# Two block products of the next gate and up pair, issued before the last plain group of what precedes them

## The chip, the cores and the metric

The kernel runs on one core of a Trainium2 chip. The metric is device time in microseconds for one execution of the whole layer. Beside it stands one execution recorded by the hardware profiler. Five engines appear: TensorE (PE in the rows, and PEld for its weight loads), VectorE (DVE), ScalarE (ACT), GpSimd (POOL) and SyncE (SP). SP issues the loads from memory, POOL issues a second kind of DMA that adds one buffer to another.

## The reference

One decoder layer in float32 for 256 tokens of width 2048. It is a half step of SwiGLU, then a mixer of dilated attention and gated linear attention, then cross-attention, then a second half step of SwiGLU. The change touches the two half steps alone:

```python
def swiglu(h, w_gate, w_up, w_down):
    return (jax.nn.silu(h @ w_gate) * (h @ w_up)) @ w_down

x = x + 0.5 * swiglu(rms_norm(x, ffn1_norm[l]), ffn1_w_gate[l], ffn1_w_up[l], ffn1_w_down[l])
```

The gate and up weights are 2048 x 5632 and the down weights 5632 x 2048. The norm's gain is folded into the activations, and its per-token factor r is applied to the finished products, inside the silu and in the multiplication by the up half.

## The kernel before

**Tiles.** The 5632 hidden columns are taken in 11 blocks f of 512, and the 2048 rows in 4 groups of 512. A weight group (tile `raw`, 128 x 4 x 512, 1 MB) is loaded by SP (L132) and split into two parts: ScalarE rounds it to fp32r (`wh`, L136) and VectorE subtracts to get the remainder (`wl`, L137). TensorE then forms three products per weight, wh by the high half of the activations (L163), wl by the high half (L164), wh by the low half (L165). A plain group is 24 matmuls, for two halves of 128 tokens (`mm3`).

**Block products.** For f = 0 of a half step, gate and up are two plain projections (`proj`). For f = 1 to 10, gate and up of one block are a pair (`strassen`) that saves one of eight products on the first two weight groups of both: the left and right weight groups 0 (`ral`, `rar`) and 1 (`rbl`, `rbr`) are combined, and seven block products of 12 matmuls each (`product`, L194) stand for them. Their order is x from ral; y from ral+rar; x from the sum with rbr as well; c0l from rbl; x from rar+rbr; c0r from rbr; and, between two plain groups, x from ral+rar+rbr+rbl. Here they are called x, y, s1, c0l, s2, c0r and xb1. The sums of weights are made in place, by VectorE (`add`, L212) and by DMAs from POOL's queue (`accumulate`, L216). Between products, results in PSUM are copied or subtracted: ScalarE copies x to c0l after the first product (L228) and y to `ys` after the second (L234), VectorE subtracts for c0r after s1 (L238) and for c1r after s2 (L243). After the seven products come the plain groups 2 and 3 of gate (left) and up (right): g2l, xb1, g2r, g3l, g3r.

**Order of the work.** The program is written in this order, and a scheduler places each engine's instructions. Splits, loads and small vector operations stand under a priority (`WPRI` = 200) that lets them be placed earlier than their place in the text. Each engine runs its own list in order and waits on semaphores. What limits how far ahead a split can run are the buffers: three slots each for `wh` and `wl` (so the split of a group waits for the end of the group three before it), six for `raw` in a half step, four PSUM accumulators and four further PSUM tiles for x, y and the transposes.

**After a pair.** The silu of gate (`sg`, L377), the product with up (`h`, L387) and the eight transposes (L355, `turn`, put off by two ticks of `later`) prepare the down product. The blocks are taken in parts of 4, 4 and 3; after each part follow the down products of that part, four chunks of 512 columns with one plain group for each block, and their sums are added to the residual (L394).

Of the kernel before, what the change touches and what calls it, by code (L numbers as in the profile page):

```python
# [8 lines left out]
F32 = mybir.dt.float32  # L9
# [7 lines left out]
P = 128  # L17
# [3 lines left out]
NC = D // 512  # L21
# [6 lines left out]
WPRI = 200  # L28
# [20 lines left out]
def layer_kernel(ctx: ExitStack, tc: tile.TileContext, A: dict, out: bass.AP):  # L49
    nc = tc.nc  # L50
    V, SC, G, PE, SY = nc.vector, nc.scalar, nc.gpsimd, nc.tensor, nc.sync
# [6 lines left out]
    pa = ctx.enter_context(tc.tile_pool(name="pa", bufs=4, space=PSUM))  # L58
# [83 lines left out]
    def wgroup(W, c, g, fine=None):  # L142

        raw = load(W, c, g)
        n = W.shape[-1]
        kn = W.shape[-2]
        with tc.high_priority(WPRI):
            wh, wl = split_tiles(kn, n)
            for i in range(kn if fine else 1):
                d = slice(i, i + 1) if fine else slice(0, kn)  # L150
                if fine:
                    fine(i)
                split(wh[:, d], wl[:, d], raw[:, d])
        ks = [(kn * g + kk, wh[:, kk], wl[:, kk]) for kk in range(kn)]
        yield ks[:kn // 2]
        yield ks[kn // 2:]

    def mm3(acc, lhs, half, first, last, ts=range(TT), seeded=False):

        for t in ts:  # L160
            for i, (k, wh, wl) in enumerate(half):
                lh, ll = lhs(k, t)
                PE.matmul(acc[t], lh, wh, start=first and i == 0, stop=False, skip_group_check=seeded)  # L163
                PE.matmul(acc[t], lh, wl, start=False, stop=False, skip_group_check=seeded)  # L164
                PE.matmul(acc[t], ll, wh, start=False, stop=last and i == len(half) - 1, skip_group_check=seeded)  # L165
# [22 lines left out]
    def product(acc, lhs, w, start):  # L188

        wh, wl = w  # L190
        first = start
        for i, j, w in ((0, 0, wh), (1, 0, wh), (0, 1, wl)):
            for k in range(4):
                PE.matmul(acc, lhs(k)[i], w[:, k], start=first, stop=j == 1 and k == 3, skip_group_check=not start)  # L194
                first = False
        tick()

    def strassen(Wl, cl, Wr, cr, lhs, ab, sums, groups):

        a, b = ab  # L200
        ral, rar = load(Wl, cl, a), load(Wr, cr, a)
        rbr, rbl = load(Wr, cr, b), load(Wl, cl, b)

        def parts(src):
            with tc.high_priority(WPRI):
                wh, wl = split_tiles(4, 512)
                split(wh, wl, src)
            return wh, wl

        def add(dst, x, y):  # L210
            with tc.high_priority(WPRI):
                V.tensor_add(dst, x, y)  # L212

        def accumulate(dst, x):
            with tc.high_priority(WPRI):
                G.dma_start(dst, x, accum_op=ALU.add)  # L216

        def of(g, t):
            return lambda k: lhs(4 * g + k, t)

        def s_(i):
            return lambda k: tuple(x[:, i, k] for x in sums)

        x, y = PM([P, 512], "x"), PM([P, 512], "y")
        c0l, c0r, c1r = (pa.tile([P, 512], F32, tag="acc", name="acc") for _ in range(3))
        product(x, of(a, 0), parts(ral), True)
        with tc.high_priority(WPRI):
            SC.copy(c0l, x)  # L228
        add(ral, ral, rar)
        accumulate(rar, rbr)  # L230
        product(y, s_(0), parts(ral), True)
        with tc.high_priority(WPRI):
            ys = W2([P, 512], "ys")
            SC.copy(ys, y)  # L234
        add(ral, ral, rbr)
        product(x, s_(1), parts(ral), False)
        with tc.high_priority(WPRI):
            V.tensor_sub(c0r, ys, x)  # L238
        product(c0l, of(b, 0), parts(rbl), False)
        accumulate(ral, rbl)  # L240
        product(x, s_(2), parts(rar), False)
        with tc.high_priority(WPRI):
            V.tensor_sub(c1r, ys, x)  # L243
        product(c0r, s_(3), parts(rbr), False)
        accs = ((c0l, x), (c0r, c1r))
        for i, g in enumerate(groups):
            for acc, W, c in zip(accs, (Wl, Wr), (cl, cr)):
                for h, half in enumerate(wgroup(W, c, g)):
                    mm3(acc, lhs, half, False, i == len(groups) - 1 and h == 1, seeded=True)
                    tick()  # L250
                if i == 0 and W is Wl and c == cl:
                    product(x, of(b, 1), parts(ral), False)
        return accs

    def proj(W, c, lhs, groups, fine=None, last=False):

        n = W.shape[-1]
        acc = [pa.tile([P, n], F32, tag="acc", name="acc") for _ in range(TT)]
        groups = list(groups)
        for i, g in enumerate(groups):  # L260
            if fine and i:
                fine(4 * i)
            if last and i == len(groups) - 1:
                both = [w for half in wgroup(W, c, g) for w in half]
                for t in range(TT):
# [80 lines left out]
    def ffn(pre, r, after, fine=None, last=False):  # L346
        wg, wu, wd = (A[f"{pre}_w_{n}"] for n in ("gate", "up", "down"))
        hT = {}

        def turn(f, hs):  # L350
            hi, lo = (FT("h", 8, [P, 4, S], F32R, n) for n in ("hTh", "hTl"))
            for t in range(TT):
                tp = PM([P, 4, P], "tp")
                for j in range(4):
                    PE.transpose(tp[:, j], hs[t][:, j * P:(j + 1) * P], ident)  # L355
                sl = slice(t * P, (t + 1) * P)
                split_from_psum(hi[:, :, sl], lo[:, :, sl], tp)
# [6 lines left out]
        sums = None  # L364
        for part in PARTS:
            for f in part:
                if sums is None:
                    gate = proj(wg, f, lhs_x, range(4), fine)
                    if callable(r):
                        r = r()  # L370
                else:
                    gate, upv = strassen(wg, f, wu, f, lhs_x, (0, 1), sums, (2, 3))
                sg = []
                with tc.high_priority(WPRI):
                    for t in range(TT):
                        s = W2([P, 512], "sg")
                        SC.activation(s, gate[t], AF.Silu, scale=r[:, t:t + 1])  # L377
                        sg.append(s)
                if sums is None:
                    sums = tuple(FT(n, 1, [P, 4, 4, P], F32R, n) for n in ("sh", "sl"))  # L380
                    sums_of(xT[0], xT[1], lambda i: tuple(p[:, 2 * i:2 * i + 2] for p in sums))
                    upv = proj(wu, f, lhs_x, range(4))
                hs = []
                with tc.high_priority(WPRI):
                    for t in range(TT):
                        h = W2([P, 512], "h")
                        V.scalar_tensor_tensor(h, upv[t], r[:, t:t + 1], sg[t], op0=ALU.mult, op1=ALU.mult)  # L387
                        hs.append(h)
                later(2, lambda f=f, hs=hs: turn(f, hs))
# [256 lines left out]
    for p2 in range(2):  # L646
        acc = proj(win, 8 + p2, lhs_x, range(4))
# [18 lines left out]
    for p2 in range(2):  # L666
        acc = proj(win, 10 + p2, lhs_x, range(4))
# [183 lines left out]
    acc = proj(A["xattn_w_k"], 0, lhs_mem, range(4))  # L851
# [181 lines left out]
```

## Time and profile before

| what | us |
|---|---|
| median of 3 runs | 1958.72 (1958.36 to 1960.10) |
| profiled execution | 1957.67 |
| its span, first to last instruction | 1955.9 |
| PE busy | 1925.7 (98%) |
| DVE busy | 1261.5 (64%) |
| ACT busy | 976.7 (50%) |
| PE waiting for ScalarE's `wh`, 8 times | 15.5 |
| PE waiting for VectorE's `wl`, 17 times | 7.0 |

The first rows are one number seen in three ways: runs without the profiler, the profiled execution, and the stretch of it that the trace covers; 1.8 us of the profiled execution lie outside the span. Busy shares are averages over the whole layer. What an engine waited for is listed by the instruction that waited, the instruction that released it, the sum, the count and the longest. In a timeline a row gives the start, the length, the engine, the source line, the operation with its output and inputs, the number of instructions taken together, and in brackets the idle time ahead of it with what ended it.

### The profile page before, as it was taken

What the parts mean: (1) busy time and instruction counts of PE and PEld (TensorE: products, weight loads), DVE (VectorE), ACT (ScalarE), POOL (GpSimd) and SP (SyncE); (2) the same over time, 40 slices, a digit from 0 to 9 for tenths busy, and PEclk for the clock granted to TensorE, in tenths of its full rate; (3) what the DMA queues carried; (4) which work ended last, traced back from release to release, by engine and by line L of the source; (5) the groups of instructions that cost most, each with busy time, mean ns of one, the idle gap of its engine ahead of it and who ended that gap; (6) DMA issues with size and microseconds to landing.
All of it is one profiled execution on the core that took longest, in us unless ns stands there. A gap on an engine that the chain in (4) does not pass through costs nothing.

```text
span 1955.9 us, 21245 instructions
## 1 busy us (share of the span) xinstructions
PE 1925.7 (98%) x8760; PEld 1586.1 (81%) x8760; DVE 1261.5 (64%) x947; ACT 976.7 (50%) x876; POOL 98.1 (5%) x101
## 2 busy tenths in 40 slices
PE   8999999999999999999999999899999999999999
PEld 6888878888878888778888889788888788887887
DVE  7776467775578655446775555677746777457863
ACT  6555345553356446444566445545534555335642
POOL 2000000000000000012221000000000000000000
PEclk9999999999999999999999999899999999999999
DMA  9677557775567734445456553567755777556771
GB/s 368 234 236 258 191 146 265 273 267 192 173 222 236 281 127 161 153 169 189 172 215 215 185 182 144 204 228 248 253 193 150 258 271 267 211 177 215 237 284 60
DMA packets 63292, 416.13 MB, mean 213 GB/s; under 512 B 7099, under 2 KB 8251, under 8 KB 14428
## 3 DMA queue, kind: packets, MB, share of 16 engines
q1 hardware_dynamic: 56284, 370.74, 49.6%
q0 software_dynamic: 5760, 41.95, 10.4%
q10 hardware_dynamic: 1152, 2.10, 0.3%
q8 instruction: 68, 1.11, 0.2%
q14 instruction: 28, 0.23, 0.0%
HBM read 370.72 MB, written 2.10 MB: 191 GB/s over the span
## 4 chain that ended last, share of the span: by engine, by line
PE 74%; DVE 16%; ACT 6%; issue 4%; DMA 1%; POOL 0%; SPq 0%; ACTq 0%; DVEq 0%
PE acc L164 20%; PE acc L165 20%; PE acc L163 20%; DVE wl L137 10%; ACT wh L136 5%; PE x L194 5%; DVE raw L212 4%; PE acc L194 1%; PE x L165 1%; PE x L164 1%; PE x L163 1%; DVE h L387 1%; PE y L194 1%; DVE acc L238 1%; PE tp L315 0%
## 5 line engine op out<-in xcount | busy, mean ns | idle before, releaser
L137 DVE TENSOR_TENSOR wl<-raw,wh 128x2048 fp32r<-128x2048 f32 (+1 forms) x407 | 919.2, 2278 | 591.8 <-ACT wh L136 589.9
L136 ACT CAST wh<-raw 128x2048 fp32r<-128x2048 f32 (+1 forms) x407 | 762.4, 1898 | 656.2 <-PE acc L165 477.7
L163 PE MATMUL acc<-wh,xTh 128*128 128x512 f32 x1024 | 403.3, 395 | 15.5 <-ACT wh L136 15.5
L164 PE MATMUL acc<-wl,xTh 128*128 128x512 f32 x1024 | 402.9, 393 | 7.1 <-DVE wl L137 7.0
L165 PE MATMUL acc<-wh,xTl 128*128 128x512 f32 x1024 | 400.7, 391 | 0.0
L163 PE MATMUL acc<-wh,hTh 128*128 128x512 f32 x704 | 274.7, 390 | 0.0
L165 PE MATMUL acc<-wh,hTl 128*128 128x512 f32 x704 | 274.0, 389 | 0.0
L164 PE MATMUL acc<-wl,hTh 128*128 128x512 f32 x704 | 273.9, 389 | 0.0
L163 PEld LDWEIGHTS acc<-wh,xTh 128*128 128x128 f32 x1024 | 193.0, 189 | 59.0 <-ACT wh L136 18.6
L164 PEld LDWEIGHTS acc<-wl,xTh 128*128 128x128 f32 x1024 | 193.5, 189 | 55.4 <-DVE wl L137 16.1
L165 PEld LDWEIGHTS acc<-wh,xTl 128*128 128x128 f32 x1024 | 193.4, 189 | 39.8
L165 PEld LDWEIGHTS acc<-wh,hTl 128*128 128x128 f32 x704 | 132.1, 188 | 27.4
L164 PEld LDWEIGHTS acc<-wl,hTh 128*128 128x128 f32 x704 | 132.2, 188 | 27.3
L163 PEld LDWEIGHTS acc<-wh,hTh 128*128 128x128 f32 x704 | 132.2, 188 | 27.1
L216 POOL DMA_DIRECT2D raw<-raw x40 | 34.6, 865 | 1179.2 <-DVE raw L212 966.2
L212 DVE TENSOR_TENSOR raw<-raw 128x2048 f32<-128x2048 f32 x40 | 91.5, 2287 | 0.7
L165 PE MATMUL x<-wh,xTl 128*128 128x512 f32 x160 | 62.3, 389 | 0.0
L164 PE MATMUL x<-wl,xTh 128*128 128x512 f32 x160 | 62.3, 389 | 0.0
L163 PE MATMUL x<-wh,xTh 128*128 128x512 f32 x160 | 62.2, 389 | 0.0
L228 ACT COPY acc<-x 128x512 f32<-128x512 f32 x20 | 11.4, 571 | 95.6 <-PE x L194 95.6
L163 PE MATMUL acc<-wh,mTh 128*128 128x512 f32 x128 | 50.1, 392 | 0.0
L165 PE MATMUL acc<-wh,mTl 128*128 128x512 f32 x128 | 49.8, 389 | 0.0
(302 smaller groups left out, 1945.0 us busy)
## 6 DMA issues: line engine op xcount, KB each, us to landing
raw<-in_ffn_w_up_dram SPq DMA_DIRECT2D x88, 1024.0 KB, 7.0
raw<-in_ffn_w_down_dram SPq DMA_DIRECT2D x88, 1024.0 KB, 5.0
raw<-in_ffn_w_gate_dram SPq DMA_DIRECT2D x85, 1024.0 KB, 7.1
raw<-in_w_in_dram SPq DMA_DIRECT2D x48, 1024.0 KB, 4.8
raw<-raw POOLq DMA_DIRECT2D x40, 1024.0 KB, 6.9
raw<-in_w_out_dram SPq DMA_DIRECT2D x16, 1024.0 KB, 4.8
raw<-in_xattn_w_k_dram SPq DMA_DIRECT2D x4, 1024.0 KB, 5.6
raw<-in_xattn_w_q_dram SPq DMA_DIRECT2D x4, 1024.0 KB, 4.7
```

Of the source, the lines that this page charges most:

```text
L136: SC.copy(wh, src)
L137: V.tensor_sub(wl, src, wh.bitcast(F32))
L163: PE.matmul(acc[t], lh, wh, start=first and i == 0, stop=False, skip_group_check=seeded)
L164: PE.matmul(acc[t], lh, wl, start=False, stop=False, skip_group_check=seeded)
L165: PE.matmul(acc[t], ll, wh, start=False, stop=last and i == len(half) - 1, skip_group_check=seeded)
L194: PE.matmul(acc, lhs(k)[i], w[:, k], start=first, stop=j == 1 and k == 3, skip_group_check=not start)
L212: V.tensor_add(dst, x, y)
L216: G.dma_start(dst, x, accum_op=ALU.add)
L228: SC.copy(c0l, x)
L238: V.tensor_sub(c0r, ys, x)
L387: V.scalar_tensor_tensor(h, upv[t], r[:, t:t + 1], sg[t], op0=ALU.mult, op1=ALU.mult)
```

## The change

`strassen` is cut in two. A new function `head` issues the four loads of the pair, the products x and y, the copies that follow each of them, the first sum by VectorE and the first sum by DMA. It returns a function `rest` that issues everything else. A caller may now issue the head of the next pair early, through an argument `ahead`, just before the last plain group of what is running:

- within a part, the head of pair f+1 is issued before g3r, the last plain group of pair f;
- for f = 0, the head of pair 1 is issued before the last group of the up projection;
- at a down part that is not the last, the head of the next part's first pair is issued before the last group of the fourth chunk.

So each of the 20 heads of the layer is issued one plain group earlier. The accumulators for c0r and c1r are taken in `rest`. No product, load, sum or copy is added or removed.

```diff
     def strassen(Wl, cl, Wr, cr, lhs, ab, sums, groups):
 
+        state = head(Wl, cl, Wr, cr, lhs, ab, sums)
+        return state(groups)
+
+    def head(Wl, cl, Wr, cr, lhs, ab, sums):
+
         a, b = ab
         ral, rar = load(Wl, cl, a), load(Wr, cr, a)
         rbr, rbl = load(Wr, cr, b), load(Wl, cl, b)
...
         x, y = PM([P, 512], "x"), PM([P, 512], "y")
-        c0l, c0r, c1r = (pa.tile([P, 512], F32, tag="acc", name="acc") for _ in range(3))
+        c0l = pa.tile([P, 512], F32, tag="acc", name="acc")
         product(x, of(a, 0), parts(ral), True)
...
             SC.copy(ys, y)
-        add(ral, ral, rbr)
...
+        def rest(groups, ahead=None):
+            c0r, c1r = (pa.tile([P, 512], F32, tag="acc", name="acc") for _ in range(2))
+            add(ral, ral, rbr)
+            product(x, s_(1), parts(ral), False)
...
+            for i, g in enumerate(groups):
+                for acc, W, c in zip(accs, (Wl, Wr), (cl, cr)):
+                    if ahead and acc is accs[1] and i == len(groups) - 1:
+                        ahead()
+                    for h, half in enumerate(wgroup(W, c, g)):
...
-    def proj(W, c, lhs, groups, fine=None, last=False):
+    def proj(W, c, lhs, groups, fine=None, last=False, ahead=None):
...
         for i, g in enumerate(groups):
+            if ahead and i == len(groups) - 1:
+                ahead()
...
+        def begin(f):
+            heads[f] = head(wg, f, wu, f, lhs_x, (0, 1), sums)
+
         for part in PARTS:
             for f in part:
+                ahead = (lambda f=f: begin(f + 1)) if f + 1 in part else None
...
-                    gate, upv = strassen(wg, f, wu, f, lhs_x, (0, 1), sums, (2, 3))
+                    gate, upv = heads.pop(f)((2, 3), ahead)
...
-                    upv = proj(wu, f, lhs_x, range(4))
+                    upv = proj(wu, f, lhs_x, range(4), ahead=ahead)
...
-                acc = proj(wd, c, lhs_h, part, last=last and end and c == NC - 1)
+                ahead = (lambda: begin(part[-1] + 1)) if c == NC - 1 and not end else None
+                acc = proj(wd, c, lhs_h, part, last=last and end and c == NC - 1, ahead=ahead)
```

In the changed kernel the line numbers above 197 shift: the add is L217, the accumulating DMA L221, the copies L233 and L239, the subtractions L246 and L251, the silu L397, h L407, the transposes L369. Splits, matmuls of groups and matmuls of products keep L136, L137, L163 to L165 and L194.

Three places of the engines' lists, first before and then with the change. The first is VectorE in pair f = 6 of the first half step, from the subtraction for c0r onwards. `raw_2483` is the weight group of g2l, `raw_2353` that of the product c0r, `raw_2349` that of xb1. Before:

```order
L238 TENSOR_TENSOR acc_2360<-ys_2413,x_2357 128x512
L137 TENSOR_TENSOR wl_2451<-raw_2351,wh_2450 128x2048
L137 TENSOR_TENSOR wl_2468<-raw_2353,wh_2467 128x2048
L243 TENSOR_TENSOR acc_2361<-ys_2413,x_2357 128x512
L137 TENSOR_TENSOR wl_2486<-raw_2483,wh_2485 128x2048
L137 TENSOR_TENSOR wl_2514<-raw_2349,wh_2513 128x2048
```

With the change (`raw_2315` is here the group of the product c0r, `raw_2311` that of xb1):

```order
L137 TENSOR_TENSOR wl_2451<-raw_2313,wh_2450 128x2048
L246 TENSOR_TENSOR acc_2397<-ys_2357,x_2319 128x512
L137 TENSOR_TENSOR wl_2468<-raw_2315,wh_2467 128x2048
L137 TENSOR_TENSOR wl_2486<-raw_2483,wh_2485 128x2048
L251 TENSOR_TENSOR acc_2398<-ys_2357,x_2319 128x512
L289 TENSOR_TENSOR hTl_2434<-tp_2435,hTh_2433 128x4x128
L137 TENSOR_TENSOR wl_2514<-raw_2311,wh_2513 128x2048
```

The subtraction for c1r has moved behind the split of g2l; the same holds in all 20 pairs.

The second is TensorE in pair f = 4 of the first half step, the first pair after a down part: the end of the product c0r and the start of g2l. `wh_1929` and `wl_1930` belong to g2l, `wh_1975` to g2r. Before:

```order
L194 MATMUL acc_1820<-wl_1912,sh_321 128x512 x4
L163 MATMUL acc_1819<-wh_1929,xTh2_214 128x512
L163 MATMUL x_1817<-wh_1929,xTh2_214 128x512
L163 MATMUL acc_1820<-wh_1975,xTh2_214 128x512
L163 MATMUL acc_1821<-wh_1975,xTh2_214 128x512
L164 MATMUL acc_1819<-wl_1930,xTh2_214 128x512
```

With the change:

```order
L194 MATMUL acc_1857<-wl_1912,sh_321 128x512 x4
L163 MATMUL acc_1787<-wh_1929,xTh2_214 128x512
L164 MATMUL acc_1787<-wl_1930,xTh2_214 128x512
L165 MATMUL acc_1787<-wh_1929,xTl2_215 128x512
L163 MATMUL acc_1787<-wh_1929,xTh2_214 128x512
L164 MATMUL acc_1787<-wl_1930,xTh2_214 128x512
```

Before, two matmuls of g2r stood between the first two and the rest of g2l; now g2l, xb1 and g2r stand one after the other, whole. The same holds in the four pairs that follow a down part.

The third is ScalarE at the first pair (f = 1) of the first half step. `sg` are the silus of block 0, the copy is c0l from x. Before (`raw_463` is the sum for s1, `raw_469` the group of c0l):

```order
L136 CAST wh_530<-raw_463 128x2048
L377 ACTIVATE sg_317<-acc_128,r1_315 128x512
L377 ACTIVATE sg_319<-acc_129,r1_315 128x512
L228 COPY acc_473<-x_471 128x512
L136 CAST wh_547<-raw_469 128x2048
```

With the change (`raw_429` is the sum for s1, `raw_435` the group of c0l, `raw_431` the sum for s2, `raw_477` the last group of up):

```order
L136 CAST wh_479<-raw_477 128x2048
L136 CAST wh_514<-raw_429 128x2048
L136 CAST wh_531<-raw_435 128x2048
L318 ACTIVATE junk_307,ss1_290<-x3_106 128x512
L318 ACTIVATE junk_309,ss1_290<-x3_106 128x512
L136 CAST wh_564<-raw_431 128x2048
L397 ACTIVATE sg_317<-acc_128,r1_315 128x512
L397 ACTIVATE sg_319<-acc_129,r1_315 128x512
L233 COPY acc_439<-x_437 128x512
```

The casts for s1, c0l and s2 now all stand ahead of the two silus and the copy; before it was the cast for s1 alone.

More of the change, by code (lines that the diff above doesn't have):

```diff
@@ L234, in strassen @@
             SC.copy(ys, y)
-        add(ral, ral, rbr)
[L236 to L253, printed above, removed]
-    def proj(W, c, lhs, groups, fine=None, last=False):
+        def rest(groups, ahead=None):
+            c0r, c1r = (pa.tile([P, 512], F32, tag="acc", name="acc") for _ in range(2))
+            add(ral, ral, rbr)
+            product(x, s_(1), parts(ral), False)
+            with tc.high_priority(WPRI):
+                V.tensor_sub(c0r, ys, x)
+            product(c0l, of(b, 0), parts(rbl), False)
+            accumulate(ral, rbl)
+            product(x, s_(2), parts(rar), False)
+            with tc.high_priority(WPRI):
+                V.tensor_sub(c1r, ys, x)
+            product(c0r, s_(3), parts(rbr), False)
+            accs = ((c0l, x), (c0r, c1r))
+            for i, g in enumerate(groups):
[3 more added lines that the diff above has]
+                    for h, half in enumerate(wgroup(W, c, g)):
+                        mm3(acc, lhs, half, False, i == len(groups) - 1 and h == 1, seeded=True)
+                        tick()
+                    if i == 0 and W is Wl and c == cl:
+                        product(x, of(b, 1), parts(ral), False)
+            return accs
+        return rest
+    def proj(W, c, lhs, groups, fine=None, last=False, ahead=None):
         n = W.shape[-1]
@@ L364, in ffn @@
         sums = None
+        heads = {}
+        def begin(f):
+            heads[f] = head(wg, f, wu, f, lhs_x, (0, 1), sums)
         for part in PARTS:
             for f in part:
+                ahead = (lambda f=f: begin(f + 1)) if f + 1 in part else None
                 if sums is None:
```

## The prediction

> **What bounds the kernel now.** I read the page's busy times first, then the list of what TensorE waited for, then the timelines at those places.
>
> ```profile
> span 1955.9 us, 21245 instructions
> PE 1925.7 (98%) x8760; PEld 1586.1 (81%) x8760; DVE 1261.5 (64%) x947; ACT 976.7 (50%) x876; POOL 98.1 (5%) x101
> ...
> L137 DVE TENSOR_TENSOR wl<-raw,wh 128x2048 fp32r<-128x2048 f32 (+1 forms) x407 | 919.2, 2278 | 591.8 <-ACT wh L136 589.9
> L136 ACT CAST wh<-raw 128x2048 fp32r<-128x2048 f32 (+1 forms) x407 | 762.4, 1898 | 656.2 <-PE acc L165 477.7
> ...
> L212 DVE TENSOR_TENSOR raw<-raw 128x2048 f32<-128x2048 f32 x40 | 91.5, 2287 | 0.7
> ...
> raw<-in_ffn_w_up_dram SPq DMA_DIRECT2D x88, 1024.0 KB, 7.0
> ...
> raw<-raw POOLq DMA_DIRECT2D x40, 1024.0 KB, 6.9
> ```
>
> TensorE is busy for all but 30.2 us of the span (1955.9 - 1925.7), and the change takes no matmul away. All it can win is a part of those 30 us, and it can lose anything. A split costs 1.90 us on ScalarE and 2.28 on VectorE, an add 2.29, and the DMAs about 7 us to land.
>
> ```profile
> PE acc L163 <- ACT wh L136: 15.5, 8, 4.6
> PE acc L164 <- DVE wl L137: 7.0, 17, 2.1
> PE wps L428 <- DVE mhalf L422: 1.1, 1, 1.1
> PE tp L662 <- DVE o L677: 1.0, 1, 1.0
> PE x L194 <- ACT acc L228: 0.7, 1, 0.7
> ```
>
> Columns: total, times, longest. Three kinds of wait stand where the change moves something. The commonest is at the start of g2l, here in pair f = 6 of the first half step:
>
> ```profile
> 377.70 0.39 PE L163 MATMUL acc<-wh,xTh 128*128 128x512 f32 x1
> 377.93 0.39 PE L163 MATMUL x<-wh,xTh 128*128 128x512 f32 x1
> 378.51 0.50 PE L164 MATMUL acc<-wl,xTh 128*128 128x512 f32 x1 [0.19 <-DVE wl L137]
> 378.85 0.40 PE L165 MATMUL acc<-wh,xTl 128*128 128x512 f32 x1
> ```
> ```profile
> 371.17 4.49 DVE L137 TENSOR_TENSOR wl<-raw,wh 128x2048 fp32r<-128x2048 f32 x2
> 375.57 0.69 DVE L243 TENSOR_TENSOR acc<-ys,x 128x512 f32<-128x512 f32 x1
> 376.17 6.69 DVE L137 TENSOR_TENSOR wl<-raw,wh 128x2048 fp32r<-128x2048 f32 x3
> ```
>
> The subtraction for c1r (L243) waits for the end of product s2, and the split of g2l stands behind it in VectorE's list. The two need 0.69 + 2.28 us less a little overlap; product c0r covers 2.7. TensorE starts 0.58 us after the matmul before instead of 0.23, and the next start is 0.34 late instead of 0.23: 0.35 + 0.11 = 0.46 us lost. It recurs in 15 of the 20 pairs, nearly all of the 17 waits for `wl` above.
>
> **The change, part by part.** First, g2l. The new list has the split of g2l ahead of the c1r subtraction. Its slot in the ring is that of the product s1, three groups before, so it can be done when s1 has ended and two splits have been taken, about 2 us before TensorE needs it. Behind it the subtraction is done about 1 us later than s2 ends; who waits for it is g2r, which now starts 2.72 + 5.44 + 2.72 = 10.9 us after s2 ends. (A product is 12 matmuls, a plain group 24, at 0.227.) The stall goes whole: 15 x 0.46 = 6.9 us.
>
> Second, the pairs after a down part:
>
> ```profile
> 291.12 0.39 PE L163 MATMUL x<-wh,xTh 128*128 128x512 f32 x1
> 293.95 0.73 PE L163 MATMUL acc<-wh,xTh 128*128 128x512 f32 x2 [2.44 <-ACT wh L136]
> ...
> 551.52 0.73 PE L163 MATMUL acc<-wh,xTh 128*128 128x512 f32 x2 [1.55 <-ACT wh L136]
> ...
> 1518.90 0.72 PE L163 MATMUL acc<-wh,xTh 128*128 128x512 f32 x2 [1.52 <-ACT wh L136]
> ...
> 1776.48 0.73 PE L163 MATMUL acc<-wh,xTh 128*128 128x512 f32 x2 [1.54 <-ACT wh L136]
> ```
> ```profile
> 282.32 0.85 POOL L216 DMA_DIRECT2D raw<-raw  x1 [10.67 <-DVE wl L137]
> ```
> ```profile
> 290.19 3.71 ACT L136 CAST wh<-raw 128x2048 fp32r<-128x2048 f32 x2 [2.77 <-PE acc L194]
> ```
>
> TensorE's list has two matmuls of g2r after the first two of g2l. The cast of g2r is the second of the two in the ScalarE row, behind that of xb1. The cast of xb1 needs the sum that the DMA of 282.32 adds, which lands some 7 us later; so g2r's cast ends at 293.9. The place waits 293.95 - 291.12 - 0.23 = 2.60 us, and 0.16 over the bracketed idle at the other three: 1.71, 1.68, 1.70. With 0.11 for each restart this is 7.7 + 0.4 = 8.1 us. The new list has g2l whole, then xb1, then g2r. Even with the cast at the same moment, xb1 would have both its parts by about 294.3 and is wanted only at 290.9 + 5.4 = 296.3; g2r later still. I count all 8.1 as gained.
>
> Third, the head in its new place. Let T = 0 be the start of g3l; x' then runs from 5.44, y' from 8.16, g3r from 10.88. The slot of g3r in the ring of three is that of g3l, so its cast cannot start before 5.44; it ends at 7.4, the `wl` at 9.7, and TensorE wants it at 10.88 + 0.23 = 11.1. That is **1.3 us of cover, the smallest in the steady pair**, and it stands if VectorE is free at 7.4. Ahead of it stand the split of x', an add, the split of y' and an add, 4 x 2.29 = 9.2 us with one cast between. The slot of x' comes free at -5.4 (end of xb1), so these can be done at about 7.3. Nothing else is lost if this holds; where it doesn't, TensorE waits at every boundary. I take nothing, between 0 and the 1.1 us a head that rival (d) works out. The loads: four of the next pair now pass g3r's on SP's queue, and SP waits in order for free buffers. Walking the new lists with these durations, I get a shortest lead of about 10 us from issue to cast, against 7.0 to land, and for a POOL addition at least 4 us beyond its 6.9. I count both at nothing; without that cover the price would be the shortfall, some us each.
>
> Fourth, the first pair of the first half step, where I see a loss:
>
> ```profile
> 61.84 1.07 PE L194 MATMUL y<-wh,sh 128*128 128x512 f32 x4
> ...
> 63.65 1.07 PE L194 MATMUL y<-wl,sh 128*128 128x512 f32 x4
> 65.39 1.20 PE L194 MATMUL x<-wh,sh 128*128 128x512 f32 x4 [0.67 <-ACT acc L228]
> ```
> ```profile
> 61.79 1.91 ACT L136 CAST wh<-raw 128x2048 fp32r<-128x2048 f32 x1 [3.52 <-DVE r1t L335]
> 63.60 1.26 ACT L377 ACTIVATE sg<-acc,r 128x512 f32<-128x512 f32 x2
> 64.75 0.59 ACT L228 COPY acc<-x 128x512 f32<-128x512 f32 x1
> ```
> ```profile
> 62.05 0.71 POOL L331 TENSOR_TENSOR r<-r1m,mhalf 128x2 f32<-128x2 f32 x1 [5.45 <-DVE r1m L337]
> ```
>
> s1 overwrites x and so waits for the copy to c0l; the copy's PSUM buffer is one of gate's, so it waits for the silus, and these for r, ready at 62.76. Before, y ends at 63.65 + 0.91 = 64.56 and s1 starts at 65.39: 0.83 lost, 0.94 with the restart. Now x', y' and g3u (the last up group) end together at the same 64.56, but in the other order. ScalarE's list has the cast for s2 ahead of the silus, and the slot of that cast is g3u's: it can start only at 64.6. The silus then follow at 66.5 (a cast's step is 63.60 - 61.79 = 1.81), the copy at 67.65 (step 64.75 - 63.60), and it ends at 68.25. So s1 starts at 68.3, after **3.74 us of idleness**, 3.85 with the restart: 2.9 us worse than before. Queued behind the copy are only works for later products. The other half step has its r early, and I find no such wait there.
>
> Is the clock lost as well? The windows (PE busy, PEld, DVE, ACT, POOL, then the granted clock, DMA share, GB/s):
>
> ```profile
> 16.00:18.00 2.00, 1.22 (x2) 0.50 (x2) 1.63 (x2) 1.45 (x3) 1.04 (x1) 0.62 1.05 440
> 18.00:22.00 4.00, 2.30 (x5) 1.82 (x6) 4.00 (x5) 3.77 (x3) 0.52 (x1) 0.50 1.02 426
> 22.00:24.00 2.00, 2.00 (x8) 1.59 (x7) 2.00 (x1) 0.70 (x2) 2.00 (x2) 0.67 1.01 398
> ...
> 294.00:298.00 4.00, 4.00 (x18) 3.29 (x19) 2.63 (x2) 0.00 (x0) 0.00 (x0) 1.00 0.95 358
> ...
> 1232.00:1236.00 4.00, 0.00 (x0) 0.00 (x0) 4.00 (x9) 3.31 (x4) 0.70 (x1) 0.88 0.00 0
> 1236.00:1240.00 4.00, 1.56 (x3) 0.84 (x4) 4.00 (x4) 4.00 (x4) 0.00 (x0) 0.50 0.01 2
> ```
> ```profile
> 16.52 1.22 PE L163 MATMUL acc<-wh,xTh 128*128 128x512 f32 x2 [2.76 <-ACT wh L136]
> ```
>
> After the idle 2.44 us that end at 293.95 the clock is 1.00. After the 2.76 that end at 16.52 it falls to 0.62 and then 0.50, and after the longest wait of all, 4.6 us (1232 to 1236 is empty), it is 0.50 too. Idleness of 3.74 lies between the latter two, so I expect the fall. Its price: 4 us at 0.50 and 2 at 0.67 lose 2.0 + 0.7 = 2.7 of full-speed time by the first of them; bounds 0 and 4 (if 8 us ran at half). I take 2.5.
>
> [...]
>
> The sum against the profiled execution of 1957.67 (span 1955.9 and 1.8 around it): 1957.67 - 6.9 - 8.1 + 2.9 + 2.5 = 1948.1. The median of the runs shown is 1958.72, 1.05 above that execution, so I expect a median of **1949.1**.
>
> **The rivals.**
>
> (a) The clock holds at the first pair. For it: the idle stretch is one, with TensorE full on either side, like the one at 293.95. Against: two of three idle stretches in the rows went cold, one of them shorter than this. Time: 1949.1 - 2.5 = 1946.6.
>
> (b) The stalls come back in part, elsewhere: the end of an add or a c0r subtraction is late by some tenths and the new boundary takes 0.2 us or so in each of 20 pairs: 1949.1 + 4 = 1953. For it: the pair's 180 matmuls take 41 us, and VectorE has 11 splits and two adds in them, 11 x 2.28 + 2 x 2.29 = 29.7 us, in tight order. Against: the covers worked out above.
>
> (c) Nothing is won, because each pair is held by the splits and a removed wait is found again at the next group: about 1958. For it: all of the waits in the list are for splits. Against: VectorE idles 591.8 us before its splits, nearly all of it waiting for casts that themselves waited for TensorE.
>
> (d) Slower: g3r's split comes late at every head. Its cast waits for g3l, and VectorE has four works ahead. If these are finished only after 9.7 + 1.3 - 2.3 = 8.7 us, the cover is gone; one more 2.29 us step in front of it would cost 2.29 - 1.3 + 0.11 = 1.1 us at 20 heads, 22 us: 1971. It decides once each head loses more than 0.5 us, since 20 x 0.5 is about the forecast gain. For it: this group has less time between its slot and its use than any other, and the adds depend on loads of 7 us. Against: the four works can begin 5 us before T = 0.
>
> **How the numbers follow.** Forecast 0.45, (a) 0.28, (b) 0.13, (c) 0.07, (d) 0.07. A measurement of this kernel can tell 0.2%, 3.9 us, from no change. Below 1954.8 lie the forecast, (a) and most of (b): faster 0.86. (c) is the same, 0.07; (d) slower, 0.07. The range goes from 1944 (no clock loss, and the first pair costing nothing more than it does now: 1958.7 - 15.0 = 1943.7) to 1955, which takes in (b).
>
> **What would show it.** In the changed kernel's trace the wait of L164 for `wl` should keep only the waits of the first 25 us and count 2 or 3, not 17. The wait of L163 for `wh` should lose its four waits at pairs after a down part and fall from 15.5 to about 8.5. A single wait of a product for the copy at L233 should stand near 64.6 us with about 3.7 us of idleness, and the granted clock in the 4 to 8 us after it should be about 0.5; at 1.00 rival (a) is right. The distance of two x' products in a steady pair should shrink by about 0.46 us. New brackets on L163 or L164 in g3r would show (b) or (d), and new brackets at other places with the same sum (c). The forecast is wrong if the copy at 64.6 is not late, or if any wait recurs twenty times.

## The result and the profile after

The changed kernel takes **1944.30 us** in the median of 4 runs (1943.48 to 1945.52); the kernel before, on the same chip, 1959.18 (1958.36 to 1960.10). The ratio is 0.9924 with a 95% interval of 0.9907 to 0.9942: 14.9 us faster, where 9.6 were forecast. It lies inside the range, at its low end. The two profiled executions, 1957.67 and 1943.48, differ by 14.2, their spans too.

The page of the changed kernel: its head, and the shares by engine of the chain of work that ended last.

```profile
span 1941.7 us, 21272 instructions
PE 1918.0 (99%) x8760; PEld 1590.3 (82%) x8760; DVE 1267.1 (65%) x947; ACT 980.6 (51%) x876; POOL 100.2 (5%) x101
...
PE 97%; DVE 1%; ACT 1%; POOL 0%; issue 0%; DMA 0%; SPq 0%
```

TensorE stands idle 23.7 us in place of 30.2, and its busy time has shrunk too, by 7.7 us, with the same 8760 matmuls. A matmul that waited a little for its operand was counted busy for longer (in the kernel before, the matmul at 378.51 that the prediction shows takes 0.50 us, its neighbours 0.39 and 0.40): the idle brackets show only part of what a late split cost. The chain that ended last is 97% TensorE, before 74%: the splits have left it.

What TensorE waited for in the changed kernel (total, times, longest):

```profile
PE acc L163 <- ACT wh L136: 9.5, 4, 4.6
PE x L194 <- ACT acc L233: 3.6, 1, 3.6
PE acc L164 <- DVE wl L137: 3.2, 2, 2.1
```

The 15 waits at g2l are gone: the two waits for `wl` that are left are start-up waits of the two half steps. So are the four of g2r's cast, 7.05 us of idleness before. The sum for `wh` fell from 15.5 to 9.5 and not to the 8.5 forecast, because all that is left of it also belongs to the start-ups, where one wait happened to last 4.44 us in place of 2.76. One wait has grown: the c0l copy, 0.7 to 3.6. That is the picture the prediction drew.

A steady pair, read from the start of y in one pair and the next, first before, then after:

```profile
363.12 1.07 PE L194 MATMUL y<-wh,sh 128*128 128x512 f32 x4
...
405.39 0.84 PE L194 MATMUL y<-wh,sh 128*128 128x512 f32 x3
```
```profile
356.93 1.07 PE L194 MATMUL y<-wh,sh 128*128 128x512 f32 x4
...
398.64 1.07 PE L194 MATMUL y<-wh,sh 128*128 128x512 f32 x4
```

42.27 us before, 41.71 after (41.69 to 41.71 in all): a pair gained **0.57**, not 0.46.

The first pair of the first half step, TensorE, ScalarE, and the windows with the granted clock:

```profile
64.07 0.39 PE L165 MATMUL acc<-wh,xTl 128*128 128x512 f32 x1
68.10 2.07 PE L194 MATMUL x<-wh,sh 128*128 128x512 f32 x4 [3.64 <-ACT acc L233]
```
```profile
64.50 1.90 ACT L136 CAST wh<-raw 128x2048 fp32r<-128x2048 f32 x1 [3.15 <-PE acc L165]
66.30 1.26 ACT L397 ACTIVATE sg<-acc,r 128x512 f32<-128x512 f32 x2
67.45 0.60 ACT L233 COPY acc<-x 128x512 f32<-128x512 f32 x1
```
```profile
64.00:68.00 4.00, 0.46 (x3) 0.04 (x1) 1.57 (x1) 3.50 (x5) 0.00 (x0) 0.94 0.82 170
68.00:72.00 4.00, 3.90 (x11) 3.15 (x12) 2.04 (x3) 1.02 (x3) 0.00 (x0) 0.63 0.41 127
```

The cast, the silus, the copy, in the order and at nearly the times worked out (64.6, 66.5, 67.65 forecast), 3.64 us of idleness (3.74), and the half clock behind it. At 0.63 over 4 us the clock cost about 0.37 x 4 = 1.5 us, though, not 2.5.

### The profile page after: what moved, and what is told of

It is laid out like the page before. It is cut to its first block, busy times and chain, and to the rows that moved or that the text cites. A ratio compares the mean times of both kernels' runs of the same rounds, so it can differ in the third digit from the quotient of the medians.

```text
span 1941.7 us, 21272 instructions
## 1 busy us (share of the span) xinstructions
PE 1918.0 (99%) x8760; PEld 1590.3 (82%) x8760; DVE 1267.1 (65%) x947; ACT 980.6 (51%) x876; POOL 100.2 (5%) x101
## 4 chain that ended last, share of the span: by engine, by line
PE 97%; DVE 1%; ACT 1%; POOL 0%; issue 0%; DMA 0%; SPq 0%
PE acc L164 23%; PE acc L165 22%; PE acc L163 22%; PE x L194 11%; PE acc L194 6%; PE y L194 3%; PE x L165 2%; PE x L164 2%; PE x L163 2%; PE tp L369 1%; PE tp L329 0%; ACT wh L136 0%; DMA xr<-in_xT_dram 0%; DVE wl L137 0%; POOL gsr L694 0%
## 5 line engine op out<-in xcount | busy, mean ns | idle before, releaser
L137 DVE TENSOR_TENSOR wl<-raw,wh 128x2048 fp32r<-128x2048 f32 (+1 forms) x407 | 920.8, 2276 | 541.7 <-ACT wh L136 540.4
L136 ACT CAST wh<-raw 128x2048 fp32r<-128x2048 f32 (+1 forms) x407 | 769.0, 1900 | 770.2 <-PE acc L165 468.9
L163 PE MATMUL acc<-wh,xTh 128*128 128x512 f32 x1024 | 402.9, 394 | 9.5 <-ACT wh L136 9.5
L164 PE MATMUL acc<-wl,xTh 128*128 128x512 f32 x1024 | 400.6, 391 | 3.2 <-DVE wl L137 3.2
L165 PE MATMUL acc<-wh,xTl 128*128 128x512 f32 x1024 | 400.1, 391 | 0.0
L163 PE MATMUL acc<-wh,hTh 128*128 128x512 f32 x704 | 274.7, 390 | 0.0
L165 PE MATMUL acc<-wh,hTl 128*128 128x512 f32 x704 | 274.0, 389 | 0.0
L164 PE MATMUL acc<-wl,hTh 128*128 128x512 f32 x704 | 273.9, 389 | 0.0
L163 PEld LDWEIGHTS acc<-wh,xTh 128*128 128x128 f32 x1024 | 192.9, 189 | 51.5 <-ACT wh L136 10.9
L164 PEld LDWEIGHTS acc<-wl,xTh 128*128 128x128 f32 x1024 | 193.4, 189 | 45.1 <-DVE wl L137 5.6
L165 PEld LDWEIGHTS acc<-wh,xTl 128*128 128x128 f32 x1024 | 193.3, 189 | 40.1
L165 PEld LDWEIGHTS acc<-wh,hTl 128*128 128x128 f32 x704 | 132.2, 188 | 27.6
L164 PEld LDWEIGHTS acc<-wl,hTh 128*128 128x128 f32 x704 | 132.2, 188 | 27.1
L163 PEld LDWEIGHTS acc<-wh,hTh 128*128 128x128 f32 x704 | 132.2, 188 | 27.1
L221 POOL DMA_DIRECT2D raw<-raw x40 | 34.6, 865 | 1155.5 <-DVE raw L217 952.6
L217 DVE TENSOR_TENSOR raw<-raw 128x2048 f32<-128x2048 f32 x40 | 91.7, 2293 | 1.4
L163 PE MATMUL x<-wh,xTh 128*128 128x512 f32 x160 | 62.2, 389 | 0.0
L164 PE MATMUL x<-wl,xTh 128*128 128x512 f32 x160 | 62.2, 389 | 0.0
L165 PE MATMUL x<-wh,xTl 128*128 128x512 f32 x160 | 62.2, 389 | 0.0
L415 DVE SCALAR_TENSOR_TENSOR x<-acc,x 128x512 f32<-128x512 f32 x48 | 33.0, 688 | 27.2 <-PE acc L165 27.2
L163 PE MATMUL acc<-wh,mTh 128*128 128x512 f32 x128 | 50.1, 392 | 0.0
L165 PE MATMUL acc<-wh,mTl 128*128 128x512 f32 x128 | 49.8, 389 | 0.0
```

The source lines that it names most:

```text
L136: SC.copy(wh, src)
L137: V.tensor_sub(wl, src, wh.bitcast(F32))
```

## The experiments

Two theories stood against each other in most runs. One: what was won is the order of two engines' lists, which the early head merely brings about. The other: it is the time that the early head gives to the splits. Times below are medians, with their ratio to runs of the kernel before on the same chip; these ratios are known to about 0.13% (2.5 us) either way. Finer differences are read from places in the profiled executions.

**The first pair's head left in its old place** (`f1_late`).

```diff
-                    gate, upv = heads.pop(f)((2, 3), ahead)
+                    if f not in heads:
+                        begin(f)
+                    gate, upv = heads.pop(f)((2, 3), ahead)
...
-                    upv = proj(wu, f, lhs_x, range(4), ahead=ahead)
+                    upv = proj(wu, f, lhs_x, range(4), ahead=ahead if pre == "ffn2" else None)
```

> The changed kernel, with the head of the first pair of the first half step (f = 1) left where it was before: behind the up projection and the silus. Everything else keeps the early head. My theory: the early head at this one place costs 3.64 us of idleness against 0.83, and 1.4 us of half clock behind it, some 4.2 us in all; so the run comes out 4.2 us below the changed kernel, near 1940, with the wait for the c0l copy back at 0.7 us. Rival: the cost at f = 1 only moved there from the start-up (the loads and splits of the first 60 us), and shows again in f = 1 at g2l: within 1 us of the changed kernel, 1943 to 1945.

1941.00 us, ratio 0.9914 (0.9901 to 0.9928); span 1938.2, 3.5 below the changed kernel. TensorE's wait for the copy is back to the old one, and the clock is whole:

```profile
PE x L194 <- ACT acc L233: 0.7, 1, 0.7
```
```profile
64.00:68.00 4.00, 3.33 (x17) 2.41 (x17) 4.00 (x4) 4.00 (x6) 0.92 (x1) 1.00 0.02 4
```

The early head at this one place is a loss, of 3.5 us by the spans where 4.2 were expected. Read at the place itself it is the 4.2: from the end of the up projection and the two products to the first down part this run takes 120.7 us (64.73 to 185.47), the changed kernel 124.9 (64.30 to 189.21). This run's start-up was 0.4 longer.

**Gate's PSUM freed early, the head kept** (`gate_copy`): the cause of that loss, attacked from the other side.

```diff
-                        SC.activation(s, gate[t], AF.Silu, scale=r[:, t:t + 1])
+                        src = gate[t]
+                        if sums is None and pre == "ffn1":
+                            V.tensor_copy(s, src)
+                            src = s
+                        SC.activation(s, src, AF.Silu, scale=r[:, t:t + 1])
```

> The changed kernel with its early head at f = 1 too, but with gate's two PSUM buffers of block 0 copied by VectorE to SBUF as soon as they are finished; the silus then work on the copies. The c0l copy no longer waits for the silus and r. Two copies are added. My theory: the idleness of 3.64 us at f = 1 of the first half step is due to the PSUM buffer that the silus hold; it goes, and so does the half clock behind it; what stays there is a wait of about 1 us for the c0r subtraction, which waits for h to free up's buffers. 1944 less some 4 us: 1940, as with the late head, and the granted clock after 64 us is 1.00. Rival: r is late in any case and the wait only moves to h and the c0r subtraction, with the same 3 to 4 us: 1943 to 1945.

**1939.68 us**, ratio 0.9905 (0.9891 to 0.9919), the lowest median of all runs; span 1937.0, 4.7 below the changed kernel. The scheduler has now put the c0l copy ahead of the cast and the silus; it runs at 61.85, and s1 follows the last up group without a gap:

```profile
61.85 0.58 ACT L233 COPY acc<-x 128x512 f32<-128x512 f32 x1
64.67 1.91 ACT L136 CAST wh<-raw 128x2048 fp32r<-128x2048 f32 x1 [2.24 <-issue]
66.49 1.33 ACT L401 ACTIVATE sg<-sg,r 128x512 f32<-128x512 f32 x2
```
```profile
64.20 0.39 PE L165 MATMUL acc<-wh,xTl 128*128 128x512 f32 x1
64.43 1.07 PE L194 MATMUL x<-wh,sh 128*128 128x512 f32 x4
```

The silus are as late as in the changed kernel; what has changed is that the PSUM buffer which the copy needs no longer waits for them. The wait of 1 us that I expected at the c0r subtraction didn't appear: the subtraction ran from 70.15 to 70.84 beside the transposes.

**Only the c1r subtraction moved, no head early** (`sub_late`, from the kernel before).

```diff
-        with tc.high_priority(WPRI):
+        with tc.high_priority(WPRI - 25):
             V.tensor_sub(c1r, ys, x)
```

> The kernel before, with one number altered: the subtraction for c1r has its priority lowered by 25, so that VectorE's list has it behind the split of g2l; TensorE's list then has g2l whole before g2r in the four pairs after a down part as well. No head is early. My theory: the stalls are due to these two places of the lists alone, so 15 x 0.46 + 8.1 = 15.0 us go without moving a product: 1944.2, with pairs 0.46 shorter than before (41.8). Rival: the early head is what gives the splits of g2l and g2r their lead, and without it the stalls stay or move to c0r or xb1: 1952 to 1959.

1946.06 us, ratio 0.9940 (0.9927 to 0.9952): 12.1 us, the larger part of it all, by one number, and the scheduler took g2l whole in the four pairs after a down part too (there g2l still waits 0.15 to 0.21 us for its `wl`). But steady pairs are 41.90, not 41.8. TensorE and VectorE in pair f = 5 show what is left:

```profile
322.45 1.13 PE L194 MATMUL x<-wl,sh 128*128 128x512 f32 x4
323.42 0.84 PE L194 MATMUL acc<-wh,xTh 128*128 128x512 f32 x3
...
331.80 0.49 PE L164 MATMUL acc<-wl,xTh 128*128 128x512 f32 x1
332.13 0.39 PE L165 MATMUL acc<-wh,xTl 128*128 128x512 f32 x1
```
```profile
320.04 4.49 DVE L137 TENSOR_TENSOR wl<-raw,wh 128x2048 fp32r<-128x2048 f32 x2 [2.03 <-ACT wh L136]
...
325.05 6.69 DVE L137 TENSOR_TENSOR wl<-raw,wh 128x2048 fp32r<-128x2048 f32 x3
331.65 0.69 DVE L243 TENSOR_TENSOR acc<-ys,x 128x512 f32<-128x512 f32 x1
```

Four matmuls of s1 take 0.97 (322.45 to 323.42) in place of 0.91, and the second matmul of g2l is followed 0.33 later in place of 0.23. The split for s1 ends near 322.3 and is used at 322.45; that of g2l ends at 331.7 and is used at 331.80. No bracket shows a wait in this pair. Neither theory had the number right: the order of the lists holds the larger part, and some 0.2 us a pair hang on the time that the splits have.

**The transposes put behind c0l as well** (`sub_turn4`, from `sub_late`): are the 0.06 of s1 due to the transposes ahead of it?

```diff
-                later(2, lambda f=f, hs=hs: turn(f, hs))
+                later(4, lambda f=f, hs=hs: turn(f, hs))
```

> As the run with the subtraction moved, and the eight transposes of a pair put off by four ticks instead of two, so that they stand behind the product c0l as in the changed kernel, not ahead of s1. In the changed kernel a pair lost 0.57 us, 0.11 more than the stall of 0.46. My theory: these 0.11 us are the slower matmuls of s1 behind the transposes, so about 18 x 0.11 = 2.0 us go: 1942.2, with pairs of 41.7. Rival: the 0.11 us come from the head's earlier place (fewer VectorE and ScalarE works beside s1): 1944.2, pairs of 41.8.

1949.03 us, ratio 0.9954 (0.9940 to 0.9967): slower than `sub_late`, with pairs of 42.1. Both expectations fail. The row of s1 (its wait is ended by ScalarE's cast of its weights) and the cast:

```profile
361.72 0.27 PE L355 MATMUL tp<-ident,h 128*128 128x128 f32 x1
362.05 1.21 PE L194 MATMUL x<-wh,sh 128*128 128x512 f32 x4
```
```profile
360.09 3.72 ACT L136 CAST wh<-raw 128x2048 fp32r<-128x2048 f32 x2 [0.32 <-DVE raw L212]
```

The cast for s1 starts at 360.09, behind the second add, and ends at 362.0; s1 starts at 362.05. Seven of the eight transposes no longer stand ahead of s1. They had covered some 0.7 us of the split's lateness (an estimate: in `sub_late` all eight take 0.79, from 319.74 to 320.53); they were not its cause.

**One h moved behind the second add** (`sub_h`, from `sub_late`): in a steady pair the splits of s1 and all that follow come 0.7 us forward, and no product moves.

```diff
-                with tc.high_priority(WPRI):
+                with tc.high_priority(WPRI - 60 if f else WPRI):
                     for t in range(TT):
                         h = W2([P, 512], "h")
```

> The run with only the c1r subtraction moved (sub_late, pairs of 41.90 us, one matmul of s1 0.05 us late and one of g2l 0.1 us late, without a bracketed wait), and now the second of the two h works on VectorE placed behind the second add. That brings the add, and with it the splits of s1, c0l, s2, c0r and g2l, some 0.7 us forward; no product moves. My theory: those slow matmuls come from splits that end at the very moment of their use; they go, and pairs take 41.7 to 41.75 as with the early head: about 14 x 0.18 = 2.5 us less than sub_late, 1943 to 1944. Rival: the slow matmuls belong to the transposes ahead of s1 or to the place of the head: pairs of 41.9 and 1946 as before.

1942.20 us, ratio 0.9923 (0.9909 to 0.9936), against 0.9924 of the changed kernel. The steady pairs are as short as with the early head, 41.69 (start of y again):

```profile
357.80 1.07 PE L194 MATMUL y<-wh,sh 128*128 128x512 f32 x4
...
399.49 1.07 PE L194 MATMUL y<-wh,sh 128*128 128x512 f32 x4
```

So the remaining 0.2 us of a steady pair were splits that ended at the moment of their use, and 0.7 us of lead is enough there. The early head supplies that lead; it isn't the only way. That the whole time equals the changed kernel's is partly chance: this run has no loss of 4.2 at f = 1. Against `f1_late`, which has early heads and not that loss either, its span is 2.1 longer (1940.3 and 1938.2). The four pairs after a down part cost it 0.7 each: they take 41.5 where early heads give 40.8, and g2l's split still ends too late in each of them, as at f = 4:

```profile
288.99 0.50 PE L164 MATMUL acc<-wl,xTh 128*128 128x512 f32 x1 [0.19 <-DVE wl L137]
```

**Early heads at the down parts alone** (`down_only`) and **within the parts alone** (`pairs_only`). In both, f = 0 keeps the late head; in the first no `ahead` is passed to the pairs, in the second none to the down part.

```diff
-                    gate, upv = heads.pop(f)((2, 3), ahead)
+                    if f not in heads:
+                        begin(f)
+                    gate, upv = heads.pop(f)((2, 3), None)
...
-                    upv = proj(wu, f, lhs_x, range(4), ahead=ahead)
+                    upv = proj(wu, f, lhs_x, range(4))
```

> The changed kernel with early heads only at the four down parts; within the parts and at f = 0 the head stands where it stood. My theory: the four waits of g2r's cast go, 8.1 us, and the 15 waits at g2l stay: 1951.1. Rival: the pairs after a down part gain nothing by themselves, since the wait of xb1's cast for the added sum is found again one group later: 1957 to 1959.

> The changed kernel with early heads only within the parts; at the down parts and at f = 0 the head stands where it stood before. My theory: 14 pairs gain 0.57 us each, 8.0 us; the four waits at pairs after a down part stay (7.3 us on L163) and f = 1 is as before: about 1951, or 7 to 8 us above the run with the late head at f = 1. Rival: the gain within a part rests on the down parts' order as well: then less than 4 us are won, 1955 or more.

`down_only` 1948.06 us, 0.9949 (0.9936 to 0.9961), 10.1 us faster; `pairs_only` 1951.60, 0.9966 (0.9953 to 0.9978), 6.6 faster. Their waits, first `down_only`, then `pairs_only`:

```profile
PE acc L163 <- ACT wh L136: 9.0, 3, 4.5
PE acc L164 <- DVE wl L137: 6.4, 18, 2.1
```
```profile
PE acc L163 <- ACT wh L136: 16.1, 8, 4.5
PE acc L164 <- DVE wl L137: 4.2, 4, 2.6
```

Each part of the change takes away its own kind of wait and leaves the other. In `down_only` steady pairs stay at 42.27, and the four pairs after a down part gain 9.0 together, where 8.1 were expected. In `pairs_only` steady pairs are 41.70, and the pairs after a down part gain nothing; the first of them even lost 1.5, because the clock fell there, which it did not do before (last section). By the medians the two make 16.7, and the run with both but without the early head at f = 1 (`f1_late`) is 17.2 faster than the kernel before: within what the intervals tell apart, the parts add.

**Extra work on VectorE ahead of g3r's split** (`spare_half`, `spare_full`): how much cover is there?

```diff
             add(ral, ral, rbr)
+            with tc.high_priority(WPRI):
+                V.tensor_reduce(ST(1, "spare"), ral[:, 0:2].rearrange("p a b -> p (a b)"), axis=AX.X, op=ALU.add)
             product(x, s_(1), parts(ral), False)
```

(In the second the whole `ral` is summed.)

> The changed kernel with an extra VectorE work of about 1.1 us (a sum over half of a weight group, its result is not used) in every pair, placed behind the second add and so just ahead of the split of g3r. My theory: that split has 1.2 to 1.3 us of cover (in the trace it ends at 358.65 and is wanted at 359.88), so 1.1 us more cost nothing or some tenths at 20 places: 1944 to 1947. Rival: the cover is less than the rows show, because a split that ends just in time already slows a matmul by 0.1 us, or because g3r isn't the tightest place: 1 us at 20 places, 1960 or more.

> As the run before it, with the sum over the whole group, about 2.2 us. TensorE's list has two matmuls of s1 behind the first two of g3r in 14 pairs here. My theory: the cover of 1.23 us is exceeded by 1.0 us, and 20 heads lose 1.0 to 1.1 each with the restart: 1944.3 + 21 = 1965. Rival: VectorE catches up before it is needed (it stands idle for 40% of the time), the cost stays below 0.3 us a head: under 1950.

The rows that these rest on, in the changed kernel: VectorE's splits behind the second add, the first of which is g3r's, and TensorE's first use of it (the L164 row).

```profile
356.40 6.83 DVE L137 TENSOR_TENSOR wl<-raw,wh 128x2048 fp32r<-128x2048 f32 x3 [0.15 <-ACT wh L136]
```
```profile
359.65 0.39 PE L163 MATMUL acc<-wh,xTh 128*128 128x512 f32 x1
359.88 0.39 PE L164 MATMUL acc<-wl,xTh 128*128 128x512 f32 x1
```

With 1.22 us more the pairs are 41.71 to 41.75: nothing is lost there, as expected. The whole came out at 1940.88, 0.9913 (0.9898 to 0.9929), *below* the changed kernel: the extra work also changed ScalarE's list at f = 1, where the silus now stand ahead of s2's cast and the c0l copy ends at 65.35, so that the wait there is 1.1 us and the clock 1.00:

```profile
63.60 1.27 ACT L399 ACTIVATE sg<-acc,r 128x512 f32<-128x512 f32 x2 [2.39 <-POOL r L347]
64.75 0.60 ACT L233 COPY acc<-x 128x512 f32<-128x512 f32 x1
...
65.75 3.74 ACT L136 CAST wh<-raw 128x2048 fp32r<-128x2048 f32 x2
```

It wasn't meant as a test of the order of that list, but it is one: same products, same buffers, casts behind the silus, and the loss at f = 1 is gone but for 0.3 us (the distance of y in f = 1 and f = 2 is 46.95 in the changed kernel and 43.08 here).

With 2.29 us more, 1948.89, 0.9954 (0.9940 to 0.9967). The cover is exceeded, and the steady pairs are 42.1, some 0.4 longer; the second pair after a down part loses 0.9 to 2.1 each time. The cost is 8 us over `spare_half`, not the 20 expected: TensorE's list has two matmuls of s1 behind the first two of g3r, and these 0.45 us of work ran while g3r's split was finished.

```profile
357.69 0.61 PE L163 MATMUL acc<-wh,xTh 128*128 128x512 f32 x2
358.14 0.61 PE L194 MATMUL x<-wh,sh 128*128 128x512 f32 x2
358.87 0.50 PE L164 MATMUL acc<-wl,xTh 128*128 128x512 f32 x1
```

So a cover of at least 1.2 us is real and 2.3 us are beyond it; what lies beyond costs less than the shortfall.

**Only x ahead, y back behind the plain group** (`x_only`, from `gate_copy`): the product y, with its copy, moves from `head` into `rest`.

```diff
         accumulate(rar, rbr)
-        product(y, s_(0), parts(ral), True)
-        with tc.high_priority(WPRI):
-            ys = W2([P, 512], "ys")
-            SC.copy(ys, y)
 
         def rest(groups, ahead=None):
+            product(y, s_(0), parts(ral), True)
+            with tc.high_priority(WPRI):
+                ys = W2([P, 512], "ys")
+                SC.copy(ys, y)
```

> The kernel with the early gate copies, and only the first product (x, with its copy, the first add and the added sum of the DMA) issued ahead of the last plain group; y stands behind it again. My theory: what counts is that the chain of split, add, split, add begins one group earlier, and x alone starts it: pairs of 41.7, and 1940 as with both products. By the ring of slots y' can be split from the end of g3l on, and s1 has some 1.8 us of cover. Rival: with y back behind g3r the second add is late again and s1 waits as in the kernel before, 0.1 to 0.2 us a pair: 1942 to 1944.

1941.08 us, 0.9914 (0.9900 to 0.9927). Steady pairs are 41.70, as with both products; one product is enough of a lead. The median is 1.4 us above that of `gate_copy`, which the intervals can't tell apart; the trace has a stall of that size at f = 1 that `gate_copy` doesn't have, where TensorE's list again has g2r's first matmuls inside g2l:

```profile
77.02 0.39 PE L163 MATMUL x<-wh,xTh 128*128 128x512 f32 x1
78.68 0.73 PE L163 MATMUL acc<-wh,xTh 128*128 128x512 f32 x2 [1.27 <-ACT wh L136]
```

## Why the prediction was right, and where its sizes were off

The places and the causes hold; three terms of the sum were mis-sized, all to the same side, and so the forecast of 1949.1 was 4.8 us too high.

*g2l, forecast 15 x 0.46 = 6.9.* Right in kind: `sub_late` removes most of the stall in steady pairs by the order of the list alone. Too small: pairs gained 0.57, 15 x 0.57 = 8.6. The step that failed is the reading that what the brackets and one restart show is all that a late split costs. A split that ended at the moment of its use cost a little under 0.1 us more a pair at s1, in pair f = 6 of the kernel before:

```profile
368.55 1.15 PE L194 MATMUL x<-wl,sh 128*128 128x512 f32 x4
369.54 0.85 PE L194 MATMUL acc<-wh,xTh 128*128 128x512 f32 x3
```

These four matmuls take 0.99 in place of 0.91, and no bracket shows it. `sub_h` shows that this goes with 0.7 us of lead. The prediction had no term for s1.

*After a down part, forecast 8.1.* Between the starts of successive down parts the changed kernel is 4.64, 3.14, 3.75 and 3.16 us shorter. Less 0.57 for each other pair in them (3, 2, 3, 2), the four pairs gained 2.93, 2.00, 2.04 and 2.02, together 9.0. Again 0.2 a pair more. In the first of these pairs in the kernel before, some thirty matmuls between 279.8 and 296 start 0.004 to 0.03 us late; in the changed kernel none does. What delayed them is not shown.

*f = 1, forecast a loss of 2.9 + 2.5 = 5.4.* Measured 4.2: from the end of the up projection and the two products (64.56 before, 64.30 after) to the first down part (186.45, 189.21) the changed kernel takes 3.0 more, and two pairs in that stretch gave back 1.1. The wait was 3.64 (3.74 forecast), and the clock did fall, as in the likeliest case, not in rival (a). Its price was mis-sized: I took the first window's loss, which contains another idle gap. The length of the idle stretch alone, from which I expected the fall, did not decide it elsewhere (last section: 2.44 us without a fall, 2.47 with one), so that the fall itself may have been right in part by luck. The cause, that the silus hold gate's PSUM buffer and stand behind the cast, is shown by `gate_copy` and `spare_half`, which each remove it in another way.

*The rest* was in no term, and nothing shows that it is the change's: the first 64 us were 0.26 shorter, and the half clock at the start of the second half step took 0.9 less (last section), about 1.1 us of luck together; and the end behind the start of the last matmul took 0.3 longer (5.08 against 4.74). The sum is 8.6 + 9.0 - 4.2 + 1.1 - 0.3 = 14.2, as between the spans.

Rivals (b), (c) and (d) are out. No wait recurs at the pairs; the cover of g3r's split, forecast at 1.3 us (the prediction's own 11.1 - 9.7 gives 1.4), is 1.23 in the trace (split ends at 358.65, used at 359.88), and `spare_half` fills it without a loss. The price that (d) set on going beyond it was too high, as `spare_full` shows.

## What to carry to other kernels

When code is moved, ask first what it does to the order of each engine's list: here one priority number gave 12 of the 15 us without moving a product, and the order of three casts against two silus took 4 of them away again. Where an operation reads PSUM but waits for a late scalar, copy the PSUM out early; the buffer, not the arithmetic, was what the next products waited for here (3.64 us, gone in `gate_copy`). A split that ended just as it was used wasn't free here (four matmuls took 0.97 to 0.99 us in place of 0.91): compare start-to-start times with the steady pitch rather than count bracketed waits.

## What the runs showed of the hardware

The half clock that came with an idle stretch of 4.6 us lasted 10.24 us before and 6.83 after. At the start of the second half step both kernels have that stretch (4.55 us in both). Before, the clock was 0.50 to 1244 and 0.84 in the next 4 us; in the changed kernel, whose execution is there 5 us earlier, it was back 2 us sooner after the restart. First before, then after:

```profile
1240.00:1244.00 4.00, 4.00 (x10) 3.17 (x10) 4.00 (x3) 0.44 (x1) 0.00 (x0) 0.50 0.86 293
1244.00:1248.00 4.00, 4.00 (x16) 3.22 (x16) 3.11 (x6) 0.41 (x1) 0.00 (x0) 0.84 0.98 375
```
```profile
1234.00:1238.00 4.00, 3.35 (x8) 2.67 (x9) 4.00 (x3) 1.43 (x2) 0.00 (x0) 0.50 0.53 180
1238.00:1242.00 4.00, 4.00 (x19) 3.22 (x18) 3.97 (x6) 0.30 (x1) 0.00 (x0) 0.96 1.03 395
```

Matmuls ran at half clock for 5.7 us there before (1239.66 to 1245.34) and for 3.9 after (1234.65 to 1238.51), which makes 0.9 us of the difference between the two profiled executions. No product near this place was moved.

Up to the last matmul the clock stood at 0.50 from 16.49 to 23.32 us and from 1235.05 to 1245.29 before (6.83 and 10.24 us), and from 16.34 to 23.16, from 67.53 to 70.95 and from 1231.48 to 1238.31 in the changed kernel (6.83, 3.41 and 6.83 us), and at 1.00 elsewhere. Why it was 10.24 us before and 6.83 after at the start of the second half step is not shown.

In `pairs_only` the first pair after a down part has nearly the idle stretch that it had before, 2.47 us and 2.44, yet here the clock was halved, from 291.73 to 295.14 (3.41 us), where before it was 1.00:

```profile
291.88 1.22 PE L163 MATMUL acc<-wh,xTh 128*128 128x512 f32 x2 [2.47 <-ACT wh L136]
```
```profile
292.00:296.00 4.00, 4.00 (x11) 3.17 (x12) 2.56 (x2) 0.00 (x0) 0.00 (x0) 0.61 1.01 342
```

So at some 2.5 us the length of an idle stretch alone, which the prediction went by, did not decide. What did is not shown.
